# A QKV projection on one core: x loaded in K quarters and transposed on VectorE, w loaded in column chunks

## The chip, the cores and the metric

The kernel runs on one NeuronCore of one Trainium2 chip. The metric is the device time of one execution in microseconds, from the first to the last instruction of the core, as the median of several runs. Below, "span" is the same length read from the profiled run; it is 1 to 2 us shorter than the timed value.

Engine names in the profile: PE is TensorE's matmuls, PEld its weight loads, DVE is VectorE, ACT is ScalarE, POOL is GpSimd, SP is SyncE. A name with a q (ACTq, SPq) is that engine's sequencer, for instance while it issues a transfer. "L87" is a line of the kernel's source; the same statement has other line numbers in the edited kernels.

## The reference

```python
# x: (16, 512, 768) fp32, w_qkv: (768, 2304) fp32
qkv = np.matmul(x, w_qkv)
q, k, v = qkv[..., :768], qkv[..., 768:1536], qkv[..., 1536:]
return np.stack([q, k, v], axis=0).astype(np.float32)
```

So x is 8192 rows of K = 768. The kernels cut the rows into 64 row tiles of 128. All of w (7.1 MB in fp32) is kept on the chip in bf16. Each row tile needs x transposed (K on the partitions), and then 30 matmuls over six K tiles: 24 of them write 512 columns and 6 write 256.

## The kernel before

```python
    for ko in range(KT):                       # KT = 6
        w_scr = w_pool.tile([P, N3], fp32)
        nc.gpsimd.dma_start(w_scr[:], w_qkv[bass.ts(ko, P), :])       # 128 partitions x 9216 bytes
        nc.vector.tensor_copy(out=w_bf[:, ko, :], in_=w_scr[:])
    # ... emit_tps(): one 128x128 transpose on TensorE; after the sixth, the
    #     six are copied from PSUM to xT by ScalarE or VectorE in turn ...
    for mi in range(MT):                       # MT = 64 row tiles
        xT = xT_tiles.pop(mi)
        # ...
            nx_m = x_pool.tile([P, K], fp32, tag="x")
            nc.sync.dma_start(nx_m[:], x_flat[bass.ts(nmi, P), :])    # 128 partitions x 3072 bytes
            nc.scalar.activation(nx_mb[:], nx_m[:], Identity)         # cast to bf16
        # ...
        for noff, nsz in n_offs:               # 512, 512, 512, 512, 256 columns
            ops = opsum_pool.tile([P, 512], fp32, tag="o")
            for ko in range(KT):
                nc.tensor.matmul(ops[:, :nsz], xT[:, ko, :], w_bf[:, ko, noff:noff + nsz], ...)
                if have_next and ko < 2 and tps_cnt < KT:
                    emit_tps(nx_mb, nxT, tps_cnt, ...)   # the next tile's transposes, between matmuls
            nc.vector.tensor_copy(out=o_sb[:, noff:noff + nsz], in_=ops[:, :nsz])   # "eviction"
        for s in range(3):
            nc.sync.dma_start(out_flat[s, bass.ts(mi, P), :], o_sb[:, bass.ts(s, H)])
```

An "eviction" below is the copy of a finished output chunk from PSUM to SBUF. The transposes of the next row tile are written between the matmuls of this one. TensorE therefore pays for them, but it hardly waits before them (5.5 us for all 378 together, by the page below).

## Time and profile before

| | before |
|---|---|
| time, median (3 runs) | 419.22 us (419.08 to 419.31) |
| span of the profiled run | 418.5 us, clock 1.0 |
| TensorE busy | 95% of the span |
| VectorE / ScalarE busy | 54% / 19% |
| last cast of w begins / unbroken TensorE work begins | 26.7 us / 28.1 us |
| one row tile in the steady state | 6.17 us |
| load rate from 3 to 20 us | 415 GB/s |

The page of the kernel before: the busy sums, two rows of the 40 slices (each digit is the busy share of a slice of 10.5 us, in tenths), the shares of the chain of work that ended last, and three groups (busy us, mean ns of one | idle us before them and what ended most of it).

```profile
span 418.5 us, 5827 instructions
PE 397.3 (95%) x2260; PEld 210.9 (50%) x2304; DVE 224.6 (54%) x358; ACT 77.7 (19%) x97; POOL 4.0 (1%) x12
...
PE   0589999999999999999999999999999999999996
...
DMA  8968777778877767877777787787777767778444
...
PE 92%; DMA 5%; issue 1%; POOL 1%; DVE 1%; POOLq 0%
...
L113 PE MATMUL ops<-w_bf,nxT 128*128 128x512 bf16 (+1 forms) x1846 | 385.5, 358 | 1.4
L123 DVE COPY o_sb<-ops 128x512 f32<-128x512 f32 (+1 forms) x320 | 201.1, 638 | 171.3 <-PE ops L113 171.1
...
L75 PE MATMUL tps<-id_sb,nx_mb 128*128 128x128 bf16 x378 | 81.9, 223 | 5.5 <-ACT nxT L86 4.5
```

TensorE is the bound. The chain that ended last is 92% PE, and the main group of matmuls had 1.4 us of idle time before it in the whole run. The mean of 223 ns for a transpose is the length of one record, and records of neighbouring matmuls overlap. Start to start a transpose costs 0.056 us, so six of them cost 0.34 us of each 6.17 us row tile.

The chain of waits of the kernel before, at its beginning (start us, length us, what), and the windows view from 3 to 20 us (window and its length, busy time and count of PE, PEld, DVE, ACT, POOL, granted clock, DMA share, GB/s):

```profile
4.39 22.29 DMA w_scr<-in_w_qkv_dram
...
28.11 8.26 PE ops L113 x41
```

```profile
3.00:20.00 17.00, 5.86 (x32) 3.33 (x33) 4.77 (x5) 4.77 (x6) 1.92 (x4) 1.00 1.01 415
```

The start hangs on one long load at 415 GB/s, and TensorE already works during it on what has landed (5.86 us of records in this window).

### The profile page before, as it was taken

The page shows a single profiled execution, that of the slowest core. Times are in us where ns is not written, and L with a number is a line of the kernel's source. Part 1 is how long each engine was busy: PE and PEld are TensorE (multiplying, and loading weights), DVE is VectorE, ACT ScalarE, POOL GpSimd, SP SyncE. Part 2 cuts the span into 40 slices and gives each one's busy share as a digit, 9 for nine tenths or more (in the row PEclk, how much of TensorE's full clock was granted, in tenths as well). Part 3 has the DMA queues.
Part 4 walks back from the last instruction along what each step waited for, and adds up shares of the span by engine and source line. Part 5 has one row for each costly group of instructions (what it writes and reads, how often), then busy time and mean ns, then how long its engine had stood idle before and what let it go on. Part 6 is the DMA issues. An engine that isn't in the chain of part 4 may idle for free.

```text
span 418.5 us, 5827 instructions
## 1 busy us (share of the span) xinstructions
PE 397.3 (95%) x2260; PEld 210.9 (50%) x2304; DVE 224.6 (54%) x358; ACT 77.7 (19%) x97; POOL 4.0 (1%) x12
## 2 busy tenths in 40 slices
PE   0589999999999999999999999999999999999996
PEld 0245555555555555555555555555555555555553
DVE  1456555555555455555555555545555555555554
ACT  3210221221122122022112112212212221221200
POOL 3000000000000000000000000000000000000000
PEclk9999999999999999999999999999999999999999
DMA  8968777778877767877777787787777767778444
GB/s 323 423 258 314 236 257 261 223 272 261 286 219 261 268 226 283 269 246 252 256 241 258 259 285 233 256 262 231 279 263 254 248 253 245 254 267 283 197 184 194
DMA packets 37756, 108.13 MB, mean 258 GB/s; under 512 B 4192, under 2 KB 4192, under 8 KB 36960
## 3 DMA queue, kind: packets, MB, share of 16 engines
q1 hardware_dynamic: 36864, 100.68, 69.7%
q0 software_dynamic: 864, 7.08, 4.1%
q8 instruction: 18, 0.29, 0.3%
q14 instruction: 10, 0.08, 0.1%
HBM read 32.24 MB, written 75.50 MB: 257 GB/s over the span
## 4 chain that ended last, share of the span: by engine, by line
PE 92%; DMA 5%; issue 1%; POOL 1%; DVE 1%; POOLq 0%
PE ops L113 86%; PE tps L75 6%; DMA w_scr<-in_w_qkv_dram 5%; POOL w_scr L66 1%; DVE w_bf L67 0%; DVE o_sb L123 0%; POOLq L151 0%; POOL id_sb masks.py:199 0%; POOL id_sb masks.py:197 0%; POOLq masks.py:199 0%; POOLq L140 0%
## 5 line engine op out<-in xcount | busy, mean ns | idle before, releaser
L113 PE MATMUL ops<-w_bf,nxT 128*128 128x512 bf16 (+1 forms) x1846 | 385.5, 358 | 1.4
L123 DVE COPY o_sb<-ops 128x512 f32<-128x512 f32 (+1 forms) x320 | 201.1, 638 | 171.3 <-PE ops L113 171.1
L113 PEld LDWEIGHTS <-nxT 128*128 128x128 bf16 x1890 | 177.5, 98 | 168.2 <-DVE nxT L88 0.7
L75 PE MATMUL tps<-id_sb,nx_mb 128*128 128x128 bf16 x378 | 81.9, 223 | 5.5 <-ACT nxT L86 4.5
L104 ACT ACTIVATE nx_mb<-nx_m 128x768 bf16<-128x768 f32 x63 | 52.9, 839 | 152.7 <-issue 135.6
L86 ACT ACTIVATE nxT<-tps 128x768 bf16<-128x768 bf16 x31 | 25.2, 811 | 167.9 <-PE tps L75 167.9
L75 PEld LDWEIGHTS <-nx_mb 128*128 128x128 bf16 x378 | 37.4, 100 | 20.9 <-ACT nx_mb L104 4.4
L88 DVE COPY nxT<-tps 128x768 bf16<-128x768 bf16 x32 | 17.8, 557 | 2.2 <-PE tps L75 2.2
L67 DVE CAST w_bf<-w_scr 128x2304 bf16<-128x2304 f32 x6 | 8.2, 1358 | 17.2 <-DMA w_scr<-in_w_qkv_dram 17.2
L113 PE MATMUL ops<-w_bf,xT 128*128 128x512 bf16 (+1 forms) x30 | 9.4, 435 | 6.0 <-DVE w_bf L67 6.0
L113 PEld LDWEIGHTS <-xT 128*128 128x128 bf16 x30 | 3.4, 116 | 9.9 <-ACT xT L86 5.2
L75 PE MATMUL tps<-id_sb,x_mb 128*128 128x128 bf16 x6 | 0.8, 310 | 4.7 <-ACT x_mb L62 4.7
L66 POOL DMA_DIRECT2D w_scr<-in_w_qkv_dram x6 | 3.3, 556 | 0.3 <-issue 0.3
L75 PEld LDWEIGHTS <-x_mb 128*128 128x128 bf16 x6 | 0.6, 138 | 4.7 <-ACT x_mb L62 4.7
L62 ACT ACT_TABLE_LOAD x1 | 1.3, 1283 | 0.7 <-PEq L140 0.7
L62 ACT ACTIVATE x_mb<-x_m 128x768 bf16<-128x768 f32 x1 | 0.8, 842 | 1.7 <-DMA x_m<-in_x_dram 1.7
L86 ACT ACTIVATE xT<-tps 128x768 bf16<-128x768 bf16 x1 | 0.8, 792 | 0.0
masks.py:199 POOL TENSOR_SCALAR_AFFINE_SELECT id_sb<-id_sb 128x128 bf16<-128x128 bf16 x1 | 0.3, 307 | 0.1
masks.py:197 POOL MEMSET id_sb<- 128x128 bf16 x1 | 0.2, 205 | 0.3 <-POOLq L140 0.3
L140 POOL MEMSET const-bfloat16-1.0<- 128x1 bf16 x1 | 0.1, 103 | 0.0
L140 POOL MEMSET const-uint8-127<- 128x1 uint8 x1 | 0.1, 103 | 0.0
L140 POOL MEMSET const-float32-0.0<- 128x1 f32 x1 | 0.1, 100 | 0.2 <-issue 0.2
(1 smaller groups left out, 0.1 us busy)
## 6 DMA issues: line engine op xcount, KB each, us to landing
out_dram<-o_sb SPq DMA_DIRECT2D x192, 384.0 KB, 3.6
nx_m<-in_x_dram SPq DMA_DIRECT2D x63, 384.0 KB, 3.6
w_scr<-in_w_qkv_dram POOLq DMA_DIRECT2D x6, 1152.0 KB, 14.8
x_m<-in_x_dram SPq DMA_DIRECT2D x1, 384.0 KB, 3.0
```

The source lines that it names most:

```text
L62: nc.scalar.activation(x_mb0[:], x_m0[:], mybir.ActivationFunctionType.Identity)
L66: nc.gpsimd.dma_start(w_scr[:], w_qkv[bass.ts(ko, P), :])
L67: nc.vector.tensor_copy(out=w_bf[:, ko, :], in_=w_scr[:])
L75: nc.tensor.matmul(tps[:, bass.ts(ko, P)], xb_tile[:, bass.ts(ko, P)], id_sb[:], is_transpose=True, start=(ko == 0), stop=(ko == KT - 1),)
L86: nc.scalar.activation(xT_view[:], tps[:], mybir.ActivationFunctionType.Identity)
L88: nc.vector.tensor_copy(out=xT_view[:], in_=tps[:])
L104: nc.scalar.activation(nx_mb[:], nx_m[:], mybir.ActivationFunctionType.Identity)
L113: nc.tensor.matmul(ops[:, :nsz], xT[:, ko, :], w_bf[:, ko, noff:noff + nsz], start=(ko == 0), stop=(ko == KT - 1),)
L123: nc.vector.tensor_copy(out=o_sb[:, noff:noff + nsz], in_=ops[:, :nsz])
L140: nc = _bacc.Bacc("TRN2", target_bir_lowering=False, num_devices=1)
```

## The change

The intent is to take the transposes off TensorE. If quarter i of K (192 columns) of x is loaded into partitions 32i to 32i+31, a single `nc.vector.transpose` over blocks of 32x32 is to give the whole transposed row tile. The rows of w must then lie on the partitions in the same order. ScalarE takes over part of the evictions. The w load is cut into column chunks (256, then four of 512), and the first five row tiles all use a chunk before the next chunk is needed, so that TensorE should be able to start early.

```diff
+    n_offs = [(0, 256)] + [(256 + 512 * i, 512) for i in range(4)]
+    ws_pool = ...(name="ws", bufs=2)          # staging of w
+    xb_pool = ...(name="xb", bufs=3);  xT_pool = ...(name="xT", bufs=7);  ps_pool = ...(name="ps", bufs=8, PSUM)
+    def load_w(c):
+        off, sz = n_offs[c]
+        st = ws_pool.tile([P, KT, 512], fp32, name="wst")
+        for i in range(4):                                   # G = 32, KC = 192
+            nc.scalar.dma_start(
+                st[i * G:(i + 1) * G, :, :sz],
+                w_qkv[i * KC:(i + 1) * KC, off:off + sz].rearrange("(j a) n -> a j n", a=G),
+            )
+        for j in range(0, KT, 2):
+            nc.vector.tensor_copy(out=w_sb[c][:, j:j + 2, :], in_=st[:, j:j + 2, :sz])
+    def load_x(mi, count):                                   # up to four row tiles at once
+        t = x_pool.tile([P, 4, 4, KC], fp32, name="xin")
+        rows = x_flat[mi * P:(mi + count) * P, :].rearrange("(g b) k -> b g k", b=G)
+        for i in range(4):
+            dst = t[i * G:(i + 1) * G, :count].rearrange("p t g k -> p (t g) k")
+            nc.sync.dma_start(dst, rows[:, :, i * KC:(i + 1) * KC])
+    def prep(mi):
+        nc.scalar.activation(xb[:], t[:, n], copy)           # cast
+        nc.vector.transpose(
+            xt.rearrange("p j (g b) -> p g j b", b=G),
+            xb.rearrange("p g (j a) -> p g j a", a=G),
+        )
+    def mm(mi, c, o_sb, evac):
+        # ... six matmuls into ps ...
+        if evac: nc.vector.tensor_copy(out=o_sb[:, off:off + sz], in_=ps[:, :sz])
+        else:    nc.scalar.activation(o_sb[:, off:off + sz], ps[:, :sz], copy)
+    FIRST = 5
+    load_x(0, 1); load_w(0); load_x(1, 4); prep(0)
+    for c in range(1, 5): load_w(c)
+    for mi in range(1, FIRST): prep(mi)
+    load_x(FIRST, 4)
+    for c in range(5):                                       # first pass: five tiles per chunk
+        for mi in range(FIRST):
+            mm(mi, c, o_first[mi], (mi + c) % 2 == 0)
+            # ... store(mi) after the last chunk ...
+    prep(FIRST)
+    for mi in range(FIRST, MT):
+        # ... load_x of four more tiles when three or fewer are loaded ahead ...
+        if mi + 1 < MT: prep(mi + 1)
+        for c in (range(5) if mi < MT - 1 else (1, 2, 3, 4, 0)):
+            mm(mi, c, o_sb, c % 2 == 0)
+        store(mi, o_sb)
-    # ... removed: the identity matrix, the transposes on TensorE, their PSUM tile and
-    #     their copies; w by whole rows on the GpSimd queue; x by whole row tiles
```

In both kernels a scheduler, working before the run, fixes the order of the instructions on each engine, and in these runs every engine then works through its own order (in the changed kernel all of x of the row tiles 1 to 4 had landed by 17.9 us, but ScalarE cast tile 1 at 40.63 us, behind the issues that stood before it). That built order can be read without running anything, and the prediction rests on it.

More of the change, by code (lines that the diff above doesn't have):

```diff
@@ L4 @@
 import concourse.tile as tile
-from concourse import bass_utils, mybir
-from concourse.masks import make_identity
+from concourse import mybir
 from concourse._compat import with_exitstack
@@ L19 @@
     P = 128
+    G = 32
     B, T, H = x.shape
@@ L23 @@
     N3 = w_qkv.shape[1]
-    assert N3 == 3 * H
-    assert K % P == 0 and M % P == 0
     KT = K // P
+    KC = K // 4
     MT = M // P
+    fp32 = mybir.dt.float32
+    mm_dt = mybir.dt.bfloat16
+    copy = mybir.ActivationFunctionType.Identity
     x_flat = x.rearrange("b t h -> (b t) h")
     out_flat = out.rearrange("s b t h -> s (b t) h")
-    n_offs = []
-    o = 0
-    while o < N3:
-        sz = min(512, N3 - o)
-        n_offs.append((o, sz))
-        o += sz
-    bf16 = mybir.dt.bfloat16
@@ L42 @@
-    fp32 = mybir.dt.float32
-    id_pool = ctx.enter_context(tc.tile_pool(name="id", bufs=1))
-    id_sb = id_pool.tile([P, P], bf16)
-    make_identity(nc, id_sb)
-    w_pool = ctx.enter_context(tc.tile_pool(name="w", bufs=6))
+    n_offs = [(0, 256)] + [(256 + 512 * i, 512) for i in range(4)]
+    ws_pool = ctx.enter_context(tc.tile_pool(name="ws", bufs=2))
     wb_pool = ctx.enter_context(tc.tile_pool(name="wb", bufs=1))
-    w_bf = wb_pool.tile([P, KT, N3], bf16)
     x_pool = ctx.enter_context(tc.tile_pool(name="x", bufs=2))
-    xb_pool = ctx.enter_context(tc.tile_pool(name="xb", bufs=2))
@@ L54 @@
-    xT_pool = ctx.enter_context(tc.tile_pool(name="xT", bufs=3))
-    tpsum_pool = ctx.enter_context(tc.tile_pool(name="tpsum", bufs=1, space=bass.MemoryType.PSUM))
-    opsum_pool = ctx.enter_context(tc.tile_pool(name="opsum", bufs=7, space=bass.MemoryType.PSUM))
-    o_pool = ctx.enter_context(tc.tile_pool(name="o", bufs=3))
-    x_m0 = x_pool.tile([P, K], fp32, tag="x")
-    nc.sync.dma_start(x_m0[:], x_flat[bass.ts(0, P), :])
-    x_mb0 = xb_pool.tile([P, K], bf16, tag="xb")
-    nc.scalar.activation(x_mb0[:], x_m0[:], mybir.ActivationFunctionType.Identity)
@@ L64 @@
-    for ko in range(KT):
-        w_scr = w_pool.tile([P, N3], fp32)
-        nc.gpsimd.dma_start(w_scr[:], w_qkv[bass.ts(ko, P), :])
-        nc.vector.tensor_copy(out=w_bf[:, ko, :], in_=w_scr[:])
-    tps_state = {}
-    def emit_tps(xb_tile, xT_tile, ko, use_scalar):
-        if ko == 0:
-            tps_state['t'] = tpsum_pool.tile([P, KT * P], bf16, tag="t", name="tps")
-        tps = tps_state['t']
-        nc.tensor.matmul(
-            tps[:, bass.ts(ko, P)],
-            xb_tile[:, bass.ts(ko, P)],
-            id_sb[:],
-            is_transpose=True,
-            start=(ko == 0),
-            stop=(ko == KT - 1),
-        )
-        if ko == KT - 1:
-            xT_view = xT_tile.rearrange("p k m -> p (k m)")
-            if use_scalar:
-                nc.scalar.activation(xT_view[:], tps[:], mybir.ActivationFunctionType.Identity)
-            else:
-                nc.vector.tensor_copy(out=xT_view[:], in_=tps[:])
@@ L90 @@
-    xT_tiles = {}
-    xT0 = xT_pool.tile([P, KT, P], bf16, tag="xt")
-    xT_tiles[0] = xT0
-    for ko in range(KT):
-        emit_tps(x_mb0, xT0, ko, use_scalar=True)
-    for mi in range(MT):
-        xT = xT_tiles.pop(mi)
-        nmi = mi + 1
-        have_next = nmi < MT
-        if have_next:
-            nx_m = x_pool.tile([P, K], fp32, tag="x")
-            nc.sync.dma_start(nx_m[:], x_flat[bass.ts(nmi, P), :])
-            nx_mb = xb_pool.tile([P, K], bf16, tag="xb")
-            nc.scalar.activation(nx_mb[:], nx_m[:], mybir.ActivationFunctionType.Identity)
-            nxT = xT_pool.tile([P, KT, P], bf16, tag="xt")
-            xT_tiles[nmi] = nxT
-        tps_cnt = 0
-        o_sb = o_pool.tile([P, N3], fp32)
-        for noff, nsz in n_offs:
-            ops = opsum_pool.tile([P, 512], fp32, tag="o")
-            for ko in range(KT):
-                nc.tensor.matmul(
-                    ops[:, :nsz],
-                    xT[:, ko, :],
-                    w_bf[:, ko, noff:noff + nsz],
-                    start=(ko == 0),
-                    stop=(ko == KT - 1),
-                )
-                if have_next and ko < 2 and tps_cnt < KT:
-                    emit_tps(nx_mb, nxT, tps_cnt, use_scalar=(nmi % 2 == 0))
-                    tps_cnt += 1
-            nc.vector.tensor_copy(out=o_sb[:, noff:noff + nsz], in_=ops[:, :nsz])
@@ new lines @@
+    xb_pool = ctx.enter_context(tc.tile_pool(name="xb", bufs=3))
+    xT_pool = ctx.enter_context(tc.tile_pool(name="xT", bufs=7))
+    ps_pool = ctx.enter_context(tc.tile_pool(name="ps", bufs=8, space=bass.MemoryType.PSUM))
+    o_pool = ctx.enter_context(tc.tile_pool(name="o", bufs=6))
+    w_sb = [wb_pool.tile([P, KT, sz], mm_dt, name=f"w{c}") for c, (_, sz) in enumerate(n_offs)]
+    def load_w(c):
[8 more added lines that the diff above has]
+            nc.vector.tensor_copy(out=w_sb[c][:, j:j + 2, :], in_=st[:, j:j + 2, :sz])
@@ new lines @@
+    xs = {}
+    def load_x(mi, count):
[4 more added lines that the diff above has]
+            nc.sync.dma_start(dst, rows[:, :, i * KC:(i + 1) * KC])
+        for n in range(count):
+            xs[mi + n] = (t, n)
+    xT = {}
+    def prep(mi):
+        t, n = xs.pop(mi)
+        xb = xb_pool.tile([P, 4, KC], mm_dt, name="xb")
+        nc.scalar.activation(xb[:], t[:, n], copy)
+        xt = xT_pool.tile([P, KT, P], mm_dt, name="xt")
+        nc.vector.transpose(
+            xt.rearrange("p j (g b) -> p g j b", b=G),
+            xb.rearrange("p g (j a) -> p g j a", a=G),
+        )
+        xT[mi] = xt
@@ L124, with store @@
+    def mm(mi, c, o_sb, evac):
+        off, sz = n_offs[c]
+        ps = ps_pool.tile([P, 512], fp32, name="ps")
+        for j in range(KT):
+            nc.tensor.matmul(ps[:, :sz], xT[mi][:, j, :], w_sb[c][:, j, :], start=(j == 0), stop=(j == KT - 1))
+        if evac:
+            nc.vector.tensor_copy(out=o_sb[:, off:off + sz], in_=ps[:, :sz])
+        else:
+            nc.scalar.activation(o_sb[:, off:off + sz], ps[:, :sz], copy)
+    def store(mi, o_sb, parts=3):
         for s in range(3):
@@ L125 @@
             nc.sync.dma_start(out_flat[s, bass.ts(mi, P), :], o_sb[:, bass.ts(s, H)])
+    FIRST = 5
+    load_x(0, 1)
+    load_w(0)
+    load_x(1, 4)
+    prep(0)
+    for c in range(1, 5):
+        load_w(c)
+    for mi in range(1, FIRST):
+        prep(mi)
+    load_x(FIRST, 4)
+    loaded = FIRST + 4
+    o_first = [o_pool.tile([P, N3], fp32, name="o") for _ in range(FIRST)]
+    for c in range(5):
+        for mi in range(FIRST):
+            mm(mi, c, o_first[mi], (mi + c) % 2 == 0)
+            if c == 4:
+                store(mi, o_first[mi])
@@ L129 @@
+    prep(FIRST)
+    for mi in range(FIRST, MT):
+        if loaded - mi <= 3 and loaded < MT:
+            n = min(4, MT - loaded)
+            load_x(loaded, n)
+            loaded += n
+        if mi + 1 < MT:
+            prep(mi + 1)
+        o_sb = o_pool.tile([P, N3], fp32, name="o")
+        order = range(5) if mi < MT - 1 else (1, 2, 3, 4, 0)
+        for c in order:
+            mm(mi, c, o_sb, c % 2 == 0)
+        store(mi, o_sb)
 _INS = ['x', 'w_qkv']
```

## The prediction

> **What bounds the kernel now.** TensorE. The chain of waits gives it 92% of the 418.5 us span. In the timeline one row tile takes 6.17 us without a gap: 24 matmuls of 512 columns, 6 of 256, 6 transposes, start to start 0.216, 0.109 and 0.056 us. Around this lie a start of 28.1 us (the chain hangs on the load of w until 26.7, then its cast) and a tail of 4.3 us.
>
> **What goes away.** TensorE's transposes: 64 x 6 x 0.056 = 21 us, all on the critical path. A row tile would take 5.83 us, 64 of them 373 us.
>
> **What comes, and where it lands.** The totals would fit: VectorE gets 64 transposes, and half of its evictions go to ScalarE. The order is the trouble.
>
> 1. *Steady state.* In the built order VectorE's transposes come in batches of four, and from row tile 17 on each batch stands behind the last eviction (chunk 4) of the row tile before, while TensorE's next row tile needs the batch's first result. Nothing overlaps there: last matmul, eviction (about 0.2 us latency, 0.69 us), one transpose, first weight load. I estimate the transpose at 0.96 us: the trace's copies from PSUM (0.691 us for 512 columns, 0.424 for 256) give 1.04 ns per element and 0.16 us fixed[...]. That makes gaps of 1.9 us, 12 times (tiles 17, 21, ... 61): 23 us. They cancel the saving.
>
> 2. *Start.* The chunks were meant to start TensorE early. But in VectorE's order the transposes of row tiles 1 and 2 stand behind the casts of chunk 3, those of 3 and 4 behind chunk 4's. So only some 2 us of matmuls precede the landing of all w; full work starts at that landing + 2.1 us of casts + 1 us. By then about 10.6 MB are loaded (w 7.1, nine row tiles of x 3.5). At the 410 GB/s of the start of before (DMA view) w would land near 30 us. But each load now writes only 32 partitions. [...]Before has none, so its trace can't say.[...]
>
> 3. *DMA later.* Per four row tiles 4.7 MB of stores and 1.6 MB of x[...]. Near, not the bound.
>
> **Sum.** 45 (start) + 371 + 23 + 4 = 443; shaded to 441 us for a possibly better load rate. Range 427 to 456. Faster by over 2%: 4%; within 2%: 12%; slower: 84%.
>
> **What would show it.** TensorE's waits: 12 gaps near 1.9 us, released by VectorE's transposes; row tiles of 5.83 us otherwise; long waits on the transposes of tiles 1 and 3 in the start; DMA rate there well below 410 GB/s; transposes near 0.96 us; granted clock 1.
>
> **What would make it wrong.** Loads on 32 partitions at full rate (then about 430). A transpose of twice the cost (up to 455). Late loads of x, on which the in-order ScalarE and VectorE stall (slower still). If the gaps were hidden: 410 to 420.

The sum stands as it was recorded, 45 + 371 + 23 + 4 = 443, shaded to 441 us, but what its first term was worked out from is cut: the 45 us of start are the author's estimate and not shown by the trace of before, and the same holds for a DMA rate "well below 410 GB/s" and for "Near, not the bound". The other terms are worked out from that trace and the built order; among them the 0.96 us of the transpose is an estimate, which takes over the cost per element and the fixed cost of the copies from PSUM.

## The result and the profile after

The changed kernel takes **454.09 us** (453.0 to 454.78, 4 runs) against 419.25 (419.08 to 419.31, 4 runs) in the same rounds. The ratio is 1.0821, with a 95% interval of 1.0793 to 1.085. All outputs are right. A ratio here and below is the mean time of one kernel's fast runs over that of the other kernel's fast runs of the same rounds, so it is not quite the ratio of the medians quoted.

The page of the changed kernel, the same lines as before plus the granted clock:

```profile
span 453.0 us, 5038 instructions
PE 378.5 (84%) x1882; PEld 188.5 (42%) x1920; DVE 175.7 (39%) x269; ACT 126.8 (28%) x195; POOL 0.2 (0%) x4
...
PE   0100699999999898989989898989989898989996
...
PEclk9999799999999999999999999999999999999999
DMA  9999665766859588695959597896959596886844
...
PE 83%; DMA 10%; DVE 5%; issue 1%; SPq 0%; ACTq 0%; DVEq 0%
...
L87 PE MATMUL ps<-w,xt 128*128 128x512 bf16 (+1 forms) x1882 | 378.5, 361 | 70.3 <-DVE xt L77 68.4
L77 DVE STREAM_TRANSPOSE xt<-xb 128x768 bf16<-128x768 bf16 x64 | 57.5, 947 | 0.0
```

Total busy time of TensorE fell by 19 us, and VectorE is less busy than before. Still the kernel is slower: the PE row shows a start of four slices with almost nothing in it and a fifth that is half full, and after that a pattern of 9 and 8. The matmul group now has 70.3 us of idle time before it, and 68.4 of it ended with a VectorE transpose (xt). No engine is overloaded. TensorE waits for a result that is made too late.

The timeline of PE in the changed kernel (start us, length us, line, operation, count [idle just before <- what ended it]); a new row starts where the engine had stood still:

```profile
14.33 1.46 PE L87 MATMUL ps<-w,xt 128*128 128x256 bf16 x6 [14.33 <-DVE xt L77]
44.88 2.74 PE L87 MATMUL ps<-w,xt 128*128 128x256 bf16 x12 [29.09 <-DVE xt L77]
52.12 100.26 PE L87 MATMUL ps<-w,xt 128*128 128x256 bf16 x482 [4.50 <-DVE xt L77]
154.05 23.51 PE L87 MATMUL ps<-w,xt 128*128 128x256 bf16 x118 [1.67 <-DVE xt L77]
...
204.42 23.51 PE L87 MATMUL ps<-w,xt 128*128 128x256 bf16 x118 [1.89 <-DVE xt L77]
229.60 23.51 PE L87 MATMUL ps<-w,xt 128*128 128x256 bf16 x118 [1.67 <-DVE xt L77]
...
431.07 17.68 PE L87 MATMUL ps<-w,xt 128*128 128x256 bf16 x88 [1.67 <-DVE xt L77]
```

Continuous work begins at 52.1 us, 24 us later than before. From 154 us on there are 12 gaps, one in every four row tiles. The ends of matmuls are modelled, so the size of a gap is better read from starts: 229.60 - 204.42 = 25.18 us for four tiles, where four tiles without a gap take 4 x 5.83 = 23.32. A gap costs 1.86 us, and twelve cost 22.3 us.

The timeline of the changed kernel around one gap, the rows of DVE and ACT that matter:

```profile
201.98 3.26 ACT L75 ACTIVATE xb<-xin 128x768 bf16<-128x768 f32 x4
...
202.79 0.69 DVE L89 COPY o<-ps 128x512 f32<-128x512 f32 x1 [1.90 <-PE ps L87]
203.39 2.69 DVE L77 STREAM_TRANSPOSE xt<-xb 128x768 bf16<-128x768 bf16 x3
```

The first cast of the batch was under way at 201.98. But VectorE has the transposes in its order behind the eviction of the last chunk, and that eviction can only begin when TensorE has finished the row tile (202.79). Then come eviction, transpose, weight load, and TensorE starts again at 204.42. VectorE had idled 1.90 us just before the eviction. This is a matter of order, not of load.

The start of the changed kernel on VectorE, from the timeline, and the windows view over the same 17 us as before:

```profile
42.04 1.90 DVE L57 CAST w<-wst 128x1024 bf16<-128x1024 f32 x3 [6.77 <-DMA wst<-in_w_qkv_dram]
43.85 1.83 DVE L77 STREAM_TRANSPOSE xt<-xb 128x768 bf16<-128x768 bf16 x2
...
49.28 1.90 DVE L57 CAST w<-wst 128x1024 bf16<-128x1024 f32 x3 [3.60 <-DMA wst<-in_w_qkv_dram]
51.09 1.83 DVE L77 STREAM_TRANSPOSE xt<-xb 128x768 bf16<-128x768 bf16 x2
```

```profile
3.00:20.00 17.00, 1.46 (x6) 0.72 (x6) 2.41 (x5) 2.12 (x2) 0.00 (x0) 1.00 1.12 233
```

The transposes of row tiles 1 and 2 stand behind the casts of w's chunk 3, and those of 3 and 4 behind chunk 4's, so the last of w holds up everything. ScalarE would have held them too: it issued transfers of w from 9.50 to 40.58 us, and its casts of the tiles 1 to 3 stood behind these issues until 40.63 (30.8 us idle in its timeline). The last of w lands at 49.2 us because the load runs at 233 GB/s instead of 415 (231 from 3 to 49 us), and because x of the tiles 5 to 8, which nobody needs yet, is loaded ahead of it (landed at 39.3). The DMA share reads 1.12 all the same (1.01 before): by this measure the DMA engines were busy throughout these 17 us in both kernels.

**The sum of the difference.** The matmuls alone need 64 x 5.83 = 373.1 us, and the transposes on TensorE before needed 64 x (6.17 - 5.83) = 21.8. What is left of the spans is 418.5 - 373.1 - 21.8 = 23.6 us before, all of it start and tail, and 453.0 - 373.1 = 79.9 us after, of which 22.3 are gaps and 57.6 start and tail. So the change saved 21.8, lost 22.3 in gaps and lost 34.0 in start and tail: together +34.5 us, the difference of the spans. The tails are alike (4.3 us). The 34.0 are mostly work that begins later, and 2.9 of them a stretch in which TensorE ran at half its rate (granted clock 0.50 from 52.1 to 58.0 us, see e_edge).

### The profile page after: what moved, and what is told of

The parts are those of the page before. It is cut to its first block, busy times and chain, and to the rows that moved or that the text cites. A ratio compares the mean times of both kernels' runs of the same rounds, so it can differ in the third digit from the quotient of the medians.

```text
span 453.0 us, 5038 instructions
## 1 busy us (share of the span) xinstructions
PE 378.5 (84%) x1882; PEld 188.5 (42%) x1920; DVE 175.7 (39%) x269; ACT 126.8 (28%) x195; POOL 0.2 (0%) x4
## 4 chain that ended last, share of the span: by engine, by line
PE 83%; DMA 10%; DVE 5%; issue 1%; SPq 0%; ACTq 0%; DVEq 0%
PE ps L87 83%; DMA xin<-in_x_dram 8%; DVE xt L77 3%; DVE o L89 2%; DMA wst<-in_w_qkv_dram 2%; DVE w L57 0%; SPq L66 0%; ACTq L52 0%; DVEq L57 0%
## 5 line engine op out<-in xcount | busy, mean ns | idle before, releaser
L87 PE MATMUL ps<-w,xt 128*128 128x512 bf16 (+1 forms) x1882 | 378.5, 361 | 70.3 <-DVE xt L77 68.4
L87 PEld LDWEIGHTS <-xt 128*128 128x128 bf16 x1920 | 188.5, 99 | 260.0 <-DVE xt L77 74.8
L89 DVE COPY o<-ps 128x512 f32<-128x512 f32 (+1 forms) x190 | 112.6, 601 | 235.6 <-PE ps L87 235.6
L91 ACT ACTIVATE o<-ps 128x512 f32<-128x512 f32 (+1 forms) x130 | 77.2, 594 | 273.7 <-PE ps L87 253.2
L75 ACT ACTIVATE xb<-xin 128x768 bf16<-128x768 f32 x64 | 50.4, 835 | 39.3 <-DMA wst<-in_w_qkv_dram 30.8
L77 DVE STREAM_TRANSPOSE xt<-xb 128x768 bf16<-128x768 bf16 x64 | 57.5, 947 | 0.0
L57 DVE CAST w<-wst 128x1024 bf16<-128x1024 f32 (+1 forms) x15 | 8.7, 635 | 37.9 <-DMA wst<-in_w_qkv_dram 37.9
```

The source lines that it names most:

```text
L57: nc.vector.tensor_copy(out=w_sb[c][:, j:j + 2, :], in_=st[:, j:j + 2, :sz])
L75: nc.scalar.activation(xb[:], t[:, n], copy)
L77: nc.vector.transpose(xt.rearrange("p j (g b) -> p g j b", b=G), xb.rearrange("p g (j a) -> p g j a", a=G),)
L87: nc.tensor.matmul(ps[:, :sz], xT[mi][:, j, :], w_sb[c][:, j, :], start=(j == 0), stop=(j == KT - 1))
L89: nc.vector.tensor_copy(out=o_sb[:, off:off + sz], in_=ps[:, :sz])
L91: nc.scalar.activation(o_sb[:, off:off + sz], ps[:, :sz], copy)
```

## The experiments

The theories:

- **A**: the twelve gaps come from the order on VectorE alone (a batch of transposes behind the last eviction), not from its load, from late x or from the cost of the transpose.
- **P**: the load is slow because each transfer writes only 32 partitions, and all of them crowd into one half of the partitions at a time (233 GB/s from 3 to 20 us, against 415 before). P gives no reason why this should be slow; no run here shows one.
- **Q**, a rival of P: the load is slow because its pieces are short (768-byte rows of x, 2048-byte rows of w, against 3072 and 9216 before).

A further letter in a quoted text means what that text says beside it. An edge, `issue_after(x)`, makes the scheduler place what is written under it behind x in the built order. It adds no new work.

| run | kernel it edits | time, us | ratio to before (95%) |
|---|---|---|---|
| e_edge | after | 431.37 | 1.0287 (1.0271 to 1.0302) |
| e_prep | after | 454.06 | 1.0825 (1.0809 to 1.0841) |
| e_start2 | after | 441.86 | 1.0535 (1.0517 to 1.0554) |
| e_halves | after | 442.32 | 1.0544 (1.0526 to 1.0562) |
| e_w128 | after | 450.69 | 1.0730 (1.0709 to 1.0750) |
| b_x32 | before | 481.74 | 1.1475 (1.1444 to 1.1505) |
| b_xq | before | 429.63 | 1.0238 (1.0208 to 1.0268) |
| e_both | after | 417.47 | 0.9932 (0.9904 to 0.9961) |
| e_best | e_w128 | 412.54 | 0.9827 (0.9809 to 0.9844) |
| e_final | e_best | 415.80 | 0.9913 (0.9896 to 0.9929) |
| e_final2 | e_final | 407.29 | 0.9704 (0.9681 to 0.9728) |
| e_final3 | e_final2 | 406.62 | 0.9683 (0.9656 to 0.9709) |

### e_edge: only the order in the steady state

```diff
-        for c in order:
-            mm(mi, c, o_sb, c % 2 == 0)
+        for n, c in enumerate(order):
+            if n >= 2 and mi + 1 < MT:
+                with tc.issue_after(made[mi + 1].ins), tc.issue_after(cast[mi + 1].ins):
+                    mm(mi, c, o_sb, c % 2 == 0)     # evictions of chunks 2 to 4 behind the next tile's
+            else:                                   # cast and transpose
+                mm(mi, c, o_sb, c % 2 == 0)
```

> Only the issue order in the steady state is changed: the evictions of chunks 2 to 4 of a row tile must be issued behind the cast and the transpose of the next row tile; loads, sizes and the start stay. Theory A (the gap of 1.86 us every fourth tile exists because VectorE's in-order queue has the transpose behind the last eviction): the 12 gaps vanish, period of four tiles 25.18 -> 23.3 us, time 454 - 22 = 432 us (430 to 434). Rival B (x comes too late, or VectorE has not the time for the transposes): the wait turns into one on the load of x or on ScalarE's cast, the period stays above 24.5 us, time above 446.

Measured: 431.37 us (430.72 to 431.89), span 430.1. The whole steady state is one row now, the last of the PE timeline of e_edge:

```profile
...
51.78 374.05 PE L88 MATMUL ps<-w,xt 128*128 128x256 bf16 x1902 [4.50 <-DVE xt L78]
```

All twelve gaps are gone, and the span is 22.9 us shorter; the gaps were reckoned at 22.3. The same transposes, evictions and loads fit under the matmuls when only their order differs, so A is shown. The run also gives a second cost as a remainder: when the row begins, 373.1 - 1.96 = 371.2 us of matmuls are left (the chunk 0 of three tiles, 0.65 us each, is done), but it takes 374.05. By the starts of the single matmuls 2.4 of these 2.9 us are a stretch at half rate at the beginning of the row (the "half-rate stretch" below): from 51.78 us twelve matmuls of 256 columns follow each other at 0.213 us instead of 0.109, then five of 512 at 0.427 instead of 0.216, and from about 57 us the full rate holds. The rest is rounding (24 x 0.216 + 6 x 0.109 is 5.838, not 5.83). The PEclk row of this run's page has only nines, so the stretch must be read from the starts. In the changed kernel it lasts from 52.1 to 58.0 us (0.213 and 0.427 us there too), costs 2.9 us and shows as the digit 7 above; the windows view gives a granted clock of 0.50 for it and 1.00 from 58 to 64 us. What brings it about was not tested.

### e_prep: the same, written earlier, order left as it is

```diff
     prep(FIRST)
+    prep(FIRST + 1)
...
-        if mi + 1 < MT:
-            prep(mi + 1)
+        if mi + 2 < MT:
+            prep(mi + 2)
```

> The program writes the cast and transpose down one row tile earlier, nothing else. In the built order of VectorE the batch of four transposes still stands behind the last eviction of the tile before the one that needs it. Theory A (issue order decides): same gaps, 12 x 1.86 us, time within 1.5 us of 454. Rival (what counts is how early the program asks for it): gaps shrink, time near 432.

Measured: 454.06 us (453.3 to 454.18). Its PE timeline has the same twelve rows, 25.18 us apart. Where in the source a piece of work is written did not matter; where the scheduler put it did.

### e_start2: the order of the start

```diff
     prep(0)
-    for c in range(1, 5):
-        load_w(c)
+    load_w(1)
     for mi in range(1, FIRST):
         prep(mi)
+    for c in range(2, 5):
+        load_w(c)
```

> Only the order in the start is changed: the casts and transposes of row tiles 1 to 4 come before chunks 2 to 4 of w. The bytes and the load rate stay. Theory A (the start lost its overlap to issue order: 50 us passed with only 3 x 0.65 us of matmuls): w4 lands still near 49 us, but only chunk 4 of five tiles is then left of the first pass, TensorE has done some 20 us of work by then: 454 - 19 = 435 us (431 to 439). Rival (the load of w alone sets the start, whatever the order): within 3 us of 454.

Measured: 441.86 us (440.74 to 442.54). The direction was right, the size was not. The edit moves the casts of x in ScalarE's order as well as the transposes in VectorE's. The transposes of the tiles 1 to 4 now came early, but new waits ate a third of the gain. The PE timeline of e_start2 over the start:

```profile
19.72 2.74 PE L87 MATMUL ps<-w,xt 128*128 128x256 bf16 x12 [4.14 <-DVE xt L77]
25.93 9.36 PE L87 MATMUL ps<-w,xt 128*128 128x256 bf16 x42 [3.47 <-DVE xt L77]
44.20 2.72 PE L87 MATMUL ps<-w,xt 128*128 128x512 bf16 x6 [8.90 <-ACT o L91]
```

ScalarE both issues the transfers of w and evicts. With the issues ahead of its evictions, those waited in line for 22.9 us, and TensorE stood 8.9 us for a PSUM buffer that ScalarE had not emptied. And the bytes ahead of chunk 4 did not stay, as the expectation had it: it landed at 56.7 us instead of 49.2, when 13.70 MB had moved instead of 10.90. By the landings in the trace x of the tiles 9 to 12 (38.0 to 44.9 us) and the first stores went ahead of it, probably because the early casts freed the buffers of x early. Here an engine that both issued transfers and worked on the data passed the wait of the one on to the other.

### e_halves: P, by spreading the same pieces over both halves

```diff
-            nc.scalar.dma_start(              # w, group i of 32 partitions
+            (nc.scalar if i < 2 else nc.sync).dma_start(
...
-            nc.sync.dma_start(dst, rows[:, :, i * KC:(i + 1) * KC])
+            (nc.scalar if i < 2 and mi <= FIRST else nc.sync).dma_start(dst, rows[:, :, i * KC:(i + 1) * KC])
```

Both kernels use two queues. In the changed kernel one carries w and the other x; here one carries what goes to the partitions 0 to 63 and the other what goes to 64 to 127. The pieces are the same.

> Same transfers, same sizes and descriptors; in the start the transfers into partitions 0-63 go on ScalarE's queue and those into 64-127 on SyncE's, so that both halves are written at once. Theory P[...]: the rate in the first 30 us rises to 300 to 400 GB/s, w lands at 28 to 36 us, time 454 - 13 to - 20 = 434 to 441 us. Rival Q (pieces of 768 and 2048 bytes, or issue and waits, set the rate): rate stays 200 to 220 GB/s, time within 3 us of 454.

Measured: 442.32 us (441.22 to 442.86). The windows view of e_halves from 3 to 20 us, and VectorE's cast of chunk 4 from its timeline:

```profile
3.00:20.00 17.00, 1.46 (x6) 0.73 (x6) 2.41 (x5) 2.12 (x2) 0.00 (x0) 1.00 1.04 293
```

```profile
35.38 1.90 DVE L57 CAST w<-wst 128x1024 bf16<-128x1024 f32 x3 [1.57 <-DMA wst<-in_w_qkv_dram]
```

The rate is 293 instead of 233 GB/s, and chunk 4's cast begins at 35.4 instead of 49.3 us. The time follows less far, because the longer steady state has one more gap (13). What held the rate at 233 was which partitions were being written at the same time, as P says, and not the length of the rows, which is the same here. It is not all of the loss: 415 was not reached.

Nor are all of the 13.9 us by which chunk 4 came earlier due to the rate. The edit also changes the order, so that x of the tiles 5 to 8 lands behind chunk 4. By the landing of chunk 4 9.37 MB had moved at 265 GB/s, in the changed kernel 10.90 MB at 222. The missing 1.53 MB at 265 GB/s are 5.8 us, so the rate accounts for about 8 (an estimate from these figures).

From 19 us on the start of the changed kernel itself mostly shows the same effect. Where by the landings its two queues write different halves (19.1 to 23.1 and 33.3 to 38.2 us), the windows view gives 266 to 277 GB/s, and where they write the same half (23.2 to 28.1 and 29.5 to 33.3), 214 to 216. One short stretch (28.1 to 29.5) and most of the time before 19 us do not sort so.

### e_w128: w over all partitions

```diff
-        for i in range(4):
-            nc.scalar.dma_start(st[i * G:(i + 1) * G, :, :sz], w_qkv[i * KC:(i + 1) * KC, ...])
+        nc.scalar.dma_start(st[:, :, :sz], w_qkv[:, off:off + sz].rearrange("(p j) n -> p j n", j=KT))
...
-        nc.scalar.activation(xb[:], t[:, n], copy)
+        nc.scalar.activation(                      # the cast puts K into the matching order
+            xb.rearrange("p g (j a) -> p g j a", a=G), t[:, n].rearrange("p g (a j) -> p g j a", a=G), copy)
```

> Each chunk of w is loaded by one transfer onto 128 partitions (partition p takes rows 6p to 6p+5; ScalarE's cast of x reads the matching order), in the same pieces of 1024 and 2048 bytes; x stays on 32-partition groups; VectorE's order is as after (transposes of tiles 1 to 4 behind the casts of chunk 4). Theory P[...]: w lands at 30 to 36 us in place of 49, time 454 - 13 to - 19 = 435 to 441 us. Rival Q (piece size, strided reads): w still lands near 49 us, time within 3 us of 454. ScalarE's strided cast should cost about the same 0.84 us.

Measured: 450.69 us (449.66 to 450.82), so the expected time was missed. The load did what P says: 303 GB/s from 3 to 20 us, chunk 4's cast at 37.6 us, full TensorE work at 40.5 us, 11.6 us earlier. Here the order is nearly that of the changed kernel (10.61 MB had moved when chunk 4 landed, against 10.90), so nearly all of this is rate. But two things were not reckoned with. The steady state of e_w128, PE timeline:

```profile
40.48 54.57 PE L90 MATMUL ps<-w,xt 128*128 128x256 bf16 x264 [24.49 <-DVE xt L80]
96.91 23.51 PE L90 MATMUL ps<-w,xt 128*128 128x256 bf16 x120 [1.86 <-DVE xt L80]
122.28 23.51 PE L90 MATMUL ps<-w,xt 128*128 128x256 bf16 x120 [1.86 <-DVE xt L80]
```

There are 14 gaps instead of 12, beginning at 96.9 us, and four tiles now take 25.38 us, so a gap costs 2.06: 28.8 us in all. And the cast that reads x in steps of six elements takes 1.55 us, against 0.84 with consecutive elements. It is hidden under matmuls in the steady state, but it is not free where it is waited for (1.56 us of e_best's chain of waits below). The sum 40.5 + 371.2 + 1.3 (only one tile's chunk 0 was done early) + 28.8 + 2.9 + 4.3 = 449.0 agrees with the span of 448.9 (the 2.9 are those of e_edge; the starts of this run give 2.5 for the half-rate stretch, the rest is the rounding).

### b_x32 and b_xq: P against Q in the kernel before

```diff
             # b_x32: four transfers of 32 partitions, whole rows of 3072 bytes
-            nc.sync.dma_start(nx_m[:], x_flat[bass.ts(nmi, P), :])
+            for i in range(4):
+                nc.sync.dma_start(nx_m[32 * i:32 * (i + 1), :], x_flat[nmi * P + 32 * i:nmi * P + 32 * (i + 1), :])
             # b_xq: four transfers of 128 partitions, rows of 768 bytes
-            nc.sync.dma_start(nx_m[:], x_flat[bass.ts(nmi, P), :])
+            for i in range(4):
+                nc.sync.dma_start(nx_m[:, 192 * i:192 * (i + 1)], x_flat[bass.ts(nmi, P), 192 * i:192 * (i + 1)])
```

> The kernel before, with each x load cut in four transfers of 32 partitions and whole rows of 3072 bytes. Theory P: while x and w load together the rate falls below the 410 GB/s of before, w lands 3 to 7 us later than 26.7 us, time 422 to 427 us; the landing of an x transfer takes longer than in the run with column quarters; DMA share in the steady state up. Rival Q (small pieces are what costs): no change, within 2 us of 419.

> The kernel before, with each x load cut in four transfers of 128 partitions and 768 bytes each: the piece size of the changed kernel without its 32 partitions. Theory P: near the kernel before, 418 to 421 us, rate in the start near 400 GB/s. Rival Q: the start's rate falls towards 207 to 300 GB/s, time 422 us or more.

Measured: b_x32 481.74 us (480.42 to 483.09), b_xq 429.63 us (428.59 to 430.55). Both expected times were missed. The rates are what these two runs are good for. First b_x32, then b_xq, in the windows view:

```profile
3.00:20.00 17.00, 6.22 (x28) 3.11 (x29) 3.28 (x3) 3.99 (x5) 1.90 (x4) 1.00 0.97 305
```

```profile
3.00:20.00 17.00, 1.87 (x11) 1.06 (x12) 1.36 (x1) 2.38 (x3) 1.91 (x4) 1.00 1.00 391
```

| run | w in the start | x in the start | GB/s, 3 to 20 us |
|---|---|---|---|
| before | 128 partitions, 9216 B | 128 partitions, 3072 B | 415 |
| b_xq | 128, 9216 B | 128, 768 B | 391 |
| b_x32 | 128, 9216 B | 32, 3072 B | 305 |
| e_w128 | 128, 2048 B | 32, 768 B | 303 |
| e_halves | 32, 2048 B, halves at once | 32, 768 B, halves at once | 293 |
| after | 32, 2048 B | 32, 768 B | 233 |

(The first chunk of w has rows of 1024 bytes where the table says 2048.) Short rows of x cost 6% of the rate (391 for 415), but this bounds Q loosely, since only 0.56 of the 6.64 MB in that window were x. Writing x by 32 partitions cost a quarter with rows of full length (305 for 415). The pieces are held fixed in e_halves and e_w128 (which also makes one transfer of w out of four), and there the rate rises. Q falls as the main cause; P stands. (For the rows of w, see e_final3.) The runs show that the partitions written at once matter most (233 against 293 GB/s with the same pieces); why they do was not shown.

The *times* of the two runs say nothing about P or Q. In b_x32 the steady state slowed as well: ScalarE waited 312.2 us for x in 60 waits, and TensorE waited 23.5 us for ScalarE's and 18.8 us for VectorE's copies of the transposes, and no run separates what about the four small transfers per row tile did that. In b_xq TensorE was busy for all of 100 to 300 us (200.00 of 200; before 198.84), and the 10 us were lost in the start, where ScalarE waited up to 12.9 us for x. The expectation had treated the cut of the transfer as free. It was not (481.74 and 429.63 us against 419).

### e_both: A and P together

e_edge and e_halves at once, nothing else.

> The changed kernel with both small edits at once, and nothing else: the order edges of e_edge in the steady state and the start transfers split by partition halves over both queues of e_halves. If theories A and P name two separate costs that add up: full TensorE work begins at about 38 us as in e_halves, no wait of TensorE on a transpose after the start, and the time is 38.2 + 371.2 + about 2.4[...] + 4.9 of tail, about 417 us (414 to 421), a ratio to before of 0.985 to 1.005. If one of the two only hid the other, the sum does not come and the time is 425 us or more.

Measured: 417.47 us (415.79 to 418.37), span 416.6, ratio 0.9932. The last row of the PE timeline of e_both:

```profile
...
38.11 373.57 PE L88 MATMUL ps<-w,xt 128*128 128x256 bf16 x1864 [2.38 <-DVE xt L78]
```

As expected: the two costs are separate and add up. (The 2.4 in the expected sum is the half-rate stretch, as measured in e_edge.) Without either, the change is about as fast as the kernel before (0.7% faster), although its full TensorE work still begins 10 us later (38.1 against 28.1).

### e_best: w128, both orders, five staging buffers

e_w128 with the edges of e_edge, five staging buffers so that no issue of w waits for a cast, and edges that put the casts of chunks 2 to 4 behind the evictions of the chunk two before.

> The three repairs together: w on 128 partitions with five staging buffers, in the start the casts of chunks 2 to 4 issued behind the transposes of tiles 1 to 4 and the evictions two chunks before, in the steady state the order of the run that removed the gaps. If the three causes are separate and complete: w lands at 29 to 34 us, then 6.5 us for chunk 4 of five tiles, 59 tiles of 5.83 us (344 us) and a tail of 5 us: 390 us (385 to 398), faster than before by 5 to 8%. If they hide each other (one common bound, such as DMA in the steady state): above 405 us.

Measured: 412.54 us (412.14 to 412.99), ratio 0.9827. It beats the kernel before by 1.7% (clear of the noise), but the expected 390 was missed by 22 us. The chain of waits of e_best:

```profile
1.38 10.89 DMA wst<-in_w_qkv_dram
12.29 15.78 DMA xin<-in_x_dram
28.23 1.56 ACT xb L79
29.81 0.99 DVE xt L85
30.85 375.44 PE ps L95 x1908
```

From 30.85 us on TensorE works without a stop; what is left to gain lies before. The expectation had x of tiles 1 to 4 landing early. It landed at 28.1 us. The transfers of w, now large and free to go, were under way at the same time, and by the chain the last transfer of this x was issued only at 12.29 us, when the second transfer of w had landed. Which of the two cost more was not tested.

### e_final, e_final2, e_final3: the start once more

e_final sends x of the tiles 0 to 4 by halves over both queues ahead of chunk 1, and holds the later chunks and tiles 5 to 8 (all on ScalarE's queue) behind the first cast. It also places the casts and transposes of the tiles 5 to 8 behind the evictions of chunk 3 (prep_behind, left out of this cut and not run alone):

```diff
-    st += [load_w(c) for c in range(1, 5)]
-    load_x(FIRST, 4)
+    st += [load_w(1)]
...
+    with tc.issue_after(cast[0].ins):
+        st += [load_w(c) for c in range(2, 5)]
+        load_x(FIRST, 4)
...
-            nc.sync.dma_start(dst, rows[:, :, i * KC:(i + 1) * KC])
+            eng = nc.scalar if mi == FIRST or (mi < FIRST and i < 2) else nc.sync
+            eng.dma_start(dst, rows[:, :, i * KC:(i + 1) * KC])
```

> The version of e_best with x of the row tiles 0 to 4 sent ahead of the second chunk of w and split by partition halves over both queues, and the later w chunks and row tiles 5 to 8 issued behind the first cast. If the start of e_best was lost to x of tiles 1 to 4 landing at 28 us behind the large w transfers (theory P with queue order): x of tiles 1 to 4 lands by about 10 to 12 us, the fifth chunk of w by about 25 to 30 us, TensorE works nearly without a gap from about 15 us, the chain after that is one piece, and the time is about 391 us (386 to 400), 5 to 8% under the kernel before. Rival: the loads as a whole, not their order, hold the start (w and x of the first five tiles must all pass at about 300 GB/s before full work): then full work begins at about 28 to 31 us as in e_best, and the time stays at 408 to 414 us.

Measured: 415.80 us (415.18 to 416.14), slower than e_best; both the expectation and the rival were missed. ScalarE in e_final's timeline:

```profile
8.34 1.55 ACT L80 ACTIVATE xb<-xin 128x768 bf16<-128x768 f32 x1
10.48 7.91 ACTq L51 DMA_DIRECT2D wst<-in_w_qkv_dram  x2
18.49 12.99 ACTq L70 DMA_DIRECT2D xin<-in_x_dram  x4
...
31.52 5.92 ACT L80 ACTIVATE xb<-xin 128x768 bf16<-128x768 f32 x4 [21.63 <-DMA wst<-in_w_qkv_dram]
```

The edge kept the issues behind the first cast, but nothing kept them behind the other four, and the scheduler put them in between. Issuing alone occupied ScalarE's sequencer until 31.5 us. So e_final2 issues those transfers on SyncE, which does no work on data in these kernels, and puts the casts of chunk 1 behind the transposes:

```diff
-        nc.scalar.dma_start(
+        (nc.scalar if c < 2 else nc.sync).dma_start(
...
-            eng = nc.scalar if mi == FIRST or (mi < FIRST and i < 2) else nc.sync
+            eng = nc.scalar if mi < FIRST and i < 2 else nc.sync
...
-    cast_w(1, st[1])
     for mi in range(1, FIRST):
         prep(mi)
+    with tc.issue_after(made[3].ins):
+        cast_w(1, st[1])
```

> e_final with the late w chunks and row tiles 5 to 8 issued on the SyncE queue, so that ScalarE holds no transfer issue behind its first cast (in e_final issues held ScalarE from 8.3 to 31.5 us and the casts of tiles 1 to 4 stood behind them), and the casts of the second w chunk put behind the transposes. If the issue order on ScalarE was what held the start of e_final: x of tiles 1 to 4 is cast as it lands, from about 12 to 18 us, the one unbroken chain of TensorE begins at about 17 to 24 us, and the time is about 398 us (391 to 407). Rival, the load as a whole holds the start: the chain begins at 30 us or has gaps that the w chunks end, and the time is 408 to 414 us.

Measured: 407.29 us (406.53 to 408.26), ratio 0.9704: 3% under the kernel before. ScalarE now cast the tiles 1 to 4 from 20.05 us on, as x landed, and not from 31.52, so the issues on its queue had held e_final. (The second edit, the edge for chunk 1's casts, was not run alone.) The time lies at the edge of the expected range, since the unbroken work began at 28.9 us and not at 17 to 24: x of the tiles 1 to 4 landed at 20 us, chunk 1 at 28.

e_final3 was meant to close one more gap, by loading tiles 9 to 12 ahead of the first stores:

```diff
+    load_x(loaded, 4)
+    loaded += 4
```

> e_final2 with x of row tiles 9 to 12 loaded before the first stores (two lines). In e_final2 TensorE stood still once after its start, from 70.4 to 79.4 us, because these tiles' loads were issued behind eighteen stores on the same queue and landed at 76.6 us. If that is all that interrupts it: one unbroken chain from about 29 us, 9 us less, about 398 us (395 to 402), a ratio to before of 0.942 to 0.957. Rival, the earlier loads push out the stores or bring the casts of tiles 9 to 12 in front of evictions: a new gap, and 403 to 408 us.

Measured: 406.62 us (405.34 to 407.15), ratio 0.9683. It is the fastest kernel, but its gain over e_final2 is far from the expected 9 us, and the rival's new gap did not come either. The expectation rested on a misreading. The PE timeline of e_final2 over the whole span, then that of e_final3:

```profile
28.85 49.74 PE L96 MATMUL ps<-w,xt 128*128 128x512 bf16 x235 [0.98 <-DVE w L60]
79.36 321.10 PE L96 MATMUL ps<-w,xt 128*128 128x256 bf16 x1617 [0.77 <-DVE xt L86]
```

```profile
28.59 370.67 PE L96 MATMUL ps<-w,xt 128*128 128x512 bf16 x1852 [0.62 <-DVE w L60]
```

The gap in e_final2 was 0.77 us. I had looked at its timeline only up to 70 us, where the row was cut by the window, and at its chain of waits, which leaves TensorE at 63 us for a detour over a store and a load and comes back at 79.36. The chain follows what released the last wait; it doesn't say that TensorE stood still on the way. The bracket with the idle time would have told it, and so would a sum: 28.85 + 49.74 + 0.77 + 321.10 leaves 4.2 us for the tail, and no room for a gap of 9.

In the start of e_final3 the rate is 327 GB/s on average from 3 to 30 us, where the kernel before had 414 from 3 to 25. That average hides two stretches. Until 20 us x of the tiles 1 to 4 is under way beside w (the last of it lands at 19.8), and the rate is 293. From 20 to 30 us only w is landing, on 128 partitions with rows of 2048 bytes:

```profile
20.00:30.00 10.00, 6.92 (x29) 3.48 (x30) 6.07 (x9) 6.38 (x6) 0.00 (x0) 1.00 1.05 385
```

So the shorter rows of w cost little (385 against 415), and what holds the rate is x. It is still written 32 partitions at a time there, with rows of 768 bytes. Which of the two it is at this point stays open; b_x32 against b_xq speaks for the partitions.

## Why the prediction was right or wrong

The direction and the reasons were right; the size was 13 us too small, near the upper end of the range (427 to 456).

- **The gaps: right.** "12 times (tiles 17, 21, ... 61): 23 us" was read from the built order alone. Measured: 12 times 1.86, 22.3 us. e_edge and e_prep show that the order is the cause.
- **The transpose: right.** 0.96 us estimated, 0.947 measured on average. The estimate took over the 1.04 ns per element and the 0.16 us fixed of the copies from PSUM, and came out 0.013 us too high.
- **The saving: right.** A row tile takes 5.83 us without the transposes, and the saving was 21.8 us (21 predicted).
- **The start: right in what held it, the size of one term off.** The text had full work wait for the landing of all of w, with loads slower than the 410 GB/s of before. So it was: the load moved 231 GB/s from 3 to 49 us, chunk 4 landed at 49.2, and full work began at 52.1 instead of the 45 used in the sum. This is the mis-sized term: 7 us. The 45 was the author's estimate. Less the text's 2.1 us of casts (1.90 measured) and 1 us, it supposes that the 10.6 MB are there at about 42 us; 10.90 MB had moved by 49.2 us, at 222 GB/s counted from zero. The two queues in the changed kernel are on different halves only part of the time; they pass through the four groups of partitions each in its own order. e_halves, where they really are on different halves, reached 293.
- **Left out: the half-rate stretch**, 2.9 us in the changed kernel, by the starts of its matmuls. The trace of before shows the same half rate (512 columns at 0.427 us until 22.3 us, then at 0.216), but hidden under the load there, so it could have been counted from that trace. It lasted from 3.8 us (e_halves) to 5.9 (the changed kernel). The prediction said "granted clock 1"; the profiled run's mean was 0.992, and 0.50 in this stretch.
- **The shading by 2 us** "for a possibly better load rate" went in the wrong direction.

Together: 7.1 in the start, 2.9 of half-rate stretch, 2 of shading and 0.5 of tail and rounding, less 0.7 in the gaps, are 11.8 of the 13.1 us. The other 1.3 are the difference between the timed value and the sum, most of it the timed value's 1.1 us over the span.

## What to carry to other kernels

Moving work to an idle engine took it off the critical path here only where it stood in the right place of that engine's order. Read the built order, and where a result is needed early, fix its place with an edge; writing it earlier in the source did nothing here (22.3 us of the loss, gone in e_edge with not one operation changed). A new layout of the loads should be costed by which partitions are written at the same moment (here 233 against 293 GB/s with the same pieces), and transfers should not be issued by an engine whose next work on data is urgent (ScalarE's casts of tiles 1 to 4 began at 31.52 us in e_final and at 20.05 in e_final2; between the two runs, of which the second has one more small edit, lie 8.5 us). Before acting on a supposed gap, read the idle time of the engine itself and check that the sum has room for it.
